# First norm, modulation and first projection of a two-layer backbone as a pipeline over channel tiles, in one written order per engine

## The chip, the cores and the metric

The kernel runs on one core of a Trainium2 chip. A core has TensorE (matrix products, PE in the rows; PEld is its load of the stationary operand), VectorE (DVE), ScalarE (ACT), GpSimd (POOL) and SyncE (SP), which here only issues DMAs. The metric is the device time of one execution in microseconds (us), as the median of several runs.

## What is computed

The reference is a backbone of two layers over 256 context tokens and 1024 latent tokens, 1024 channels wide. Only its beginning matters here:

```python
def modulate(x, shift, scale):
    return rmsnorm(x) * (1.0 + scale) + shift
...
    for layer in range(DEPTH):
        mod_l = (jax.nn.silu(c) @ w_ada[layer] + b_ada[layer])[:, None, :]
        mod_c = (jax.nn.silu(c_ctx) @ w_ada[layer] + b_ada[layer])[None, None, :]
        sh1_l, sc1_l, g1_l, sh2_l, sc2_l, g2_l = jnp.split(mod_l, 6, axis=-1)
        ...
        pl = split_proj(modulate(xl, sh1_l, sc1_l) @ w_in[layer])
        pc = split_proj(modulate(xc, sh1_c, sc1_c) @ w_in[layer])
        mixed = (hgrn2_mixer(...), mlstm_mixer(...), retention_mixer(...), gla_mixer(...))
        ...
```

`rmsnorm` divides each token by the root mean square over its 1024 channels. Four mixers (chunkwise scans), an output projection and an MLP follow in each layer.

## The kernel before

The tokens lie along the free axis, 1280 of them (256 context, then 1024 latent), in three blocks `TBS` of 256, 512 and 512; the channels lie on the partitions, in `NK` = 8 channel tiles of 128. The residual is `self.X[k]`, a tile of 128 x 1280 for each channel tile k (`x` in the rows). The normed, modulated input is kept as a sum of two parts of reduced precision, `Hhi` and `Hlo`, and weights likewise (hi and lo), so that each product of the projections is three matrix products: hi by hi, hi by lo, lo by hi. For most projections these are L294, L295 and L296 (`mm3`).

The program begins with `build`: the context block of x is loaded by ScalarE's queue, and the silu of the two conditions is made (`params`). Then the 16 tiles of shift and scale of the first norm (`mod`) come as one piece: `ada_unit` (L383) loads 32 pieces of `w_ada` (256 KB each, 512 columns) and multiplies each at once, `ada_finish` copies, transposes and adds the bias. `params2` and `cond_rows` make small tables for the mixers (some 40 operations on 4 to 24 columns).

`mix_open` then runs the first norm and the first projection of a layer. That projection is `denseVS` (L601): for each of `NC` = 10 chunks of 128 tokens it sums over the 8 channel tiles into one bank of PSUM, 304 columns wide, 3 products for each channel tile, 240 in all. ScalarE and VectorE evacuate a chunk (L604, L605). The eight weight tiles come from `w_vs`, and are split into hi on ScalarE (L591) and lo on VectorE (L592). In layer 0 the norm of each token block is `norm_mod`: `rstd` squares the eight channel tiles on ScalarE (L447), sums them by products with a tile of ones (L448, L452) and makes the inverse root by Ln and Exp (L454, L455; in its other form, where `fast` is 0, the squares L435 are summed by VectorE, L436, and one product L438 sums over the partitions; L440 and L441 are its Ln and Exp). `norm_apply` does three operations for each channel tile k of the block:

```python
            nc.vector.scalar_tensor_tensor(t, self.X[k][...], self.mod[...], r, ...)         # L477
            nc.scalar.activation(R(hi), t, AF.Identity, bias=b)                              # L480
            nc.vector.scalar_tensor_tensor(R(lo), t, b, hi, op0=ALU.add, op1=ALU.subtract)   # L482
```

The order of the instructions on each engine isn't that of the code: a scheduler of the tile framework sets it, from dependencies and a model of costs, and each engine then takes its instructions in that order. DMAs are issued by SP's queue in its order.

After the first projection, `turn` transposes part of its result (L616, evacuated by L617), and the mixers begin: small products and gates for the first mixer (L787, then L307 to L314), and beside them, as filler for TensorE, the other projections (L294 to L296, with weights split by L282 and L283).

## Time and profile before

| | |
|---|---|
| median of 3 runs | 3275.53 us (3268.72 to 3275.95) |
| the profiled execution | 3272.16 us |
| its span, from the first to the last instruction | 3270.4 us |
| PE busy | 3189.2 us (98%) |
| PEld busy | 2612.7 us (80%) |
| DVE busy | 2098.0 us (64%) |
| ACT busy | 1285.5 us (39%) |
| mean granted clock of TensorE | 0.992 |

An execution's time is a little longer than its span. Busy times are those of one profiled execution. A stretch of the granted clock is given as a share of 2.4 GHz: 1.00 is that, 0.50 is 1.2 GHz. Records of TensorE overlap, so a product's record is longer than its share of time; where many follow each other, the distance of their starts is what one costs. A product of 32-bit operands (the sums of squares, the modulation) has two records.

### The profile page before, as it was taken

The page shows a single profiled execution, that of the slowest core. Times are in us where ns is not written, and L with a number is a line of the kernel's source. Part 1 is how long each engine was busy: PE and PEld are TensorE (multiplying, and loading weights), DVE is VectorE, ACT ScalarE, POOL GpSimd, SP SyncE. Part 2 cuts the span into 40 slices and gives each one's busy share as a digit, 9 for nine tenths or more (in the row PEclk, how much of TensorE's full clock was granted, in tenths as well). Part 3 has the DMA queues.
Part 4 walks back from the last instruction along what each step waited for, and adds up shares of the span by engine and source line. Part 5 has one row for each costly group of instructions (what it writes and reads, how often), then busy time and mean ns, then how long its engine had stood idle before and what let it go on. Part 6 is the DMA issues. An engine that isn't in the chain of part 4 may idle for free.

```text
span 3270.4 us, 52561 instructions
## 1 busy us (share of the span) xinstructions
PE 3189.2 (98%) x20681; PEld 2612.7 (80%) x20681; DVE 2098.0 (64%) x4333; ACT 1285.5 (39%) x2665; POOL 11.5 (0%) x42
## 2 busy tenths in 40 slices
PE   7999999999999999999999999999999999999998
PEld 4787788877888888888888677788778888888887
DVE  4778887776588845454545586876756555555546
ACT  4666564546332121212122575764544322222222
POOL 0000000000000000000000000000000000000000
PEclk9999899999999999999999999999999999999999
DMA  5115565345157511111111222333324111111111
GB/s 208 60 60 178 180 187 195 117 135 183 57 164 232 161 39 39 39 39 39 39 39 40 78 66 71 118 108 115 94 71 149 58 48 49 46 52 46 52 49 65
DMA packets 181953, 308.20 MB, mean 94 GB/s; under 512 B 21880, under 2 KB 51240, under 8 KB 181448
## 3 DMA queue, kind: packets, MB, share of 16 engines
q1 hardware_dynamic: 180376, 303.02, 28.7%
q8 instruction: 162, 2.65, 0.3%
q10 hardware_dynamic: 1296, 1.81, 0.2%
q14 instruction: 87, 0.71, 0.1%
q0 software_dynamic: 32, 0.01, 0.0%
HBM read 259.11 MB, written 45.65 MB: 93 GB/s over the span
## 4 chain that ended last, share of the span: by engine, by line
PE 84%; DVE 6%; DMA 5%; ACT 3%; issue 1%; SPq 0%; DVEq 0%; ACTq 0%
PE psum L294 22%; PE psum L295 22%; PE psum L296 22%; PE psum L831 2%; PE psum L601 2%; PE psum L632 1%; PE psum L834 1%; PE psum L818 1%; PE psum L634 1%; PE psum L633 1%; PE psum L1019 1%; PE psum L706 1%; DMA ph<-w_adaR 1%; PE psum L1358 1%; DVE px L991 1%
## 5 line engine op out<-in xcount | busy, mean ns | idle before, releaser
L526 DVE SCALAR_TENSOR_TENSOR x<-psum,st,x 128x512 f32<-128x512 f32 (+1 forms) x648 | 440.4, 689 | 204.3 <-PE psum L296 203.8
L282 ACT ACTIVATE pc<-st 128x512 fp32r<-128x512 f32 x256 | 161.3, 632 | 853.5 <-PE psum L295 841.3
L295 PE MATMUL psum<-pc,pc 128*128 128x512 f32 (+1 forms) x1296 | 477.1, 368 | 5.0 <-DVE pc L506 5.0
L294 PE MATMUL psum<-pc,pc 128*128 128x512 f32 (+1 forms) x1296 | 476.3, 368 | 0.0
L296 PE MATMUL psum<-pc,pc 128*128 128x512 f32 (+1 forms) x1296 | 474.9, 366 | 0.0
L294 PE MATMUL psum<-Hhi,pc 128*128 128x512 f32 (+1 forms) x1280 | 471.1, 368 | 1.6 <-ACT pc L282 1.5
L295 PE MATMUL psum<-Hlo,pc 128*128 128x512 f32 (+1 forms) x1280 | 472.0, 369 | 0.1
L296 PE MATMUL psum<-Hhi,pc 128*128 128x512 f32 (+1 forms) x1280 | 470.5, 368 | 0.0
L294 PE MATMUL psum<-Hhi,pw 128*128 128x512 f32 (+1 forms) x1192 | 450.8, 378 | 8.3 <-ACT pw L282 3.9
L296 PE MATMUL psum<-Hhi,pw 128*128 128x512 f32 (+1 forms) x1192 | 447.5, 376 | 0.6 <-DVE pw L283 0.6
L295 PE MATMUL psum<-Hlo,pw 128*128 128x512 f32 (+1 forms) x1192 | 446.5, 375 | 0.0
L505 DVE TENSOR_TENSOR st<-st 128x256 f32<-128x256 f32 (+1 forms) x160 | 101.8, 636 | 301.5 <-ACT pc L504 300.8
L295 PEld LDWEIGHTS psum<-pc,pc 128*128 128x128 f32 x1296 | 245.1, 189 | 47.0 <-DVE pc L506 5.5
L294 PEld LDWEIGHTS psum<-pc,pc 128*128 128x128 f32 x1296 | 245.1, 189 | 44.2 <-DVE x L526 1.3
L296 PEld LDWEIGHTS psum<-pc,pc 128*128 128x128 f32 x1296 | 244.7, 189 | 43.0 <-issue 2.7
L294 PEld LDWEIGHTS psum<-Hhi,pc 128*128 128x128 f32 x1280 | 241.3, 189 | 43.3 <-ACT pc L282 2.4
L295 PEld LDWEIGHTS psum<-Hlo,pc 128*128 128x128 f32 x1280 | 241.3, 189 | 40.9 <-issue 0.5
L283 DVE TENSOR_TENSOR pc<-st,pc 128x512 fp32r<-128x512 f32 x256 | 175.6, 689 | 153.3 <-ACT pc L282 133.4
L296 PEld LDWEIGHTS psum<-Hhi,pc 128*128 128x128 f32 x1280 | 241.1, 188 | 41.0 <-DVE pc L283 0.6
L294 PEld LDWEIGHTS psum<-Hhi,pw 128*128 128x128 f32 x1192 | 227.3, 191 | 54.4 <-issue 9.6
L296 PEld LDWEIGHTS psum<-Hhi,pw 128*128 128x128 f32 x1192 | 227.2, 191 | 39.4 <-issue 2.6
L295 PEld LDWEIGHTS psum<-Hlo,pw 128*128 128x128 f32 x1192 | 227.6, 191 | 37.2 <-issue 2.2
(401 smaller groups left out, 4868.6 us busy)
## 6 DMA issues: line engine op xcount, KB each, us to landing
st<-w_ff SPq DMA_DIRECT2D x256, 256.0 KB
ph<-w_adaR SPq DMA_DIRECT2D x128, 256.0 KB
st<-w_inT SPq DMA_DIRECT2D x96, 256.0 KB
st<-w_adaR SPq DMA_DIRECT2D x74, 256.0 KB
pc<-w_adaR SPq DMA_DIRECT2D x54, 256.0 KB
st<-w_out SPq DMA_DIRECT2D x50, 256.0 KB
d_z<-st SPq DMA_DIRECT2D x40, 256.0 KB
ps<-w_ada SPq DMA_DIRECT2D x32, 256.0 KB
```

Of the source, the lines that this page charges most:

```text
L282: nc.scalar.activation(hi, raw, AF.Copy)
L283: (eng or nc.vector).tensor_tensor(lo, raw, F(hi), op=ALU.subtract)
L294: t.matmul(out, lhsT=w[0], rhs=m[0], start=first, stop=False)
L295: t.matmul(out, lhsT=w[0], rhs=m[1], start=False, stop=False)
L296: t.matmul(out, lhsT=w[1], rhs=m[0], start=False, stop=last)
L505: nc.vector.tensor_tensor(r, r, r, op=ALU.mult)
L526: nc.vector.scalar_tensor_tensor(x, ps, self.mod[:, l, 40 + o, j:j + 1], x, op0=ALU.mult, op1=ALU.add)
L601: t.matmul(ps[:, 0:304], lhsT=h[a], rhs=u[b], start=(k + i == 0), stop=(k == NK - 1 and i == 2))
L632: t.matmul(ps[:, e, :], lhsT=h[0], rhs=u[0], start=(k == 0), stop=False)
L633: t.matmul(ps[:, e, :], lhsT=h[0], rhs=u[1], start=False, stop=False)
L634: t.matmul(ps[:, e, :], lhsT=h[1], rhs=u[0], start=False, stop=(k == NK - 1))
L831: nc.tensor.matmul(o, lhsT=ST[r0:r0 + kd, c, d, :], rhs=qd[d](c)[r0:r0 + kd, :], start=(j == 0), stop=False, tile_position=(r0, 0))
```

## The change

In layer 0, the modulation, the norm and the first projection become one function, `open_first`, written in the order in which each engine is to run it: the block `manual_schedule` keeps the code's order on every engine for what stands in it. The projection's inner piece is taken out as `part(c, k, bank)`: three products of chunk c with channel tile k; the loop over k is now outside the loop over the chunks, so six banks of PSUM are summed side by side. The first two token blocks (768 tokens, chunks 0 to 5) go through together: for each pair q of channel tiles come the quarter of the modulation that they need (`w_ada` is laid out anew, in four quarters of 8 pieces of 256 KB), two weight tiles, the norm's three operations (now L428, L430, L431) and the products (L665). The third block follows as a second pass over k with chunks 6 to 9. All loads are issued by SP. The sums of squares use `rstd` in its other form for all three blocks (its squares are now L508 and L511, its adds L512, its product L514, its Ln and Exp L516 and L517). `params2` and `cond_rows` are called at the end of `mix_open`. In layer 1 the same instructions come as before.

```diff
-    def ada_unit(self, l, r, k, bank, bufs):
...
-    def ada_finish(self, l, r, bank, bank2, tmp):
...
+    def open_first(self, vs):
+        nc, io, hp = self.nc, self.io, self.heap
+        aring = Ring([hp.alloc(512) for _ in range(10)])
+        two = CTX + 512
+        rs = {}
+        def load_x(a, b):
+            for k in range(NK):
+                nc.sync.dma_start(self.X[k][:, a:b], io["xT"][:, k, a:b])
+        def load_w(q):
+            out = []
+            for k in range(NK):
+                w = aring.next()(4, 128)
+                nc.sync.dma_start(w, io["w_ada"][q, k])
+                out.append(w)
+            return out
+        def products(ws):
+            for k in range(NK):
+                for g in range(4):
+                    nc.tensor.matmul(self.bank(6)[32 * g:32 * g + 32, 0:128], lhsT=self.cc[:, k, :], rhs=ws[k][:, g, :],
+                                     start=(k == 0), stop=(k == NK - 1), tile_position=(0, 32 * g))
+            s = self.tmps.items[6](128)
+            nc.scalar.activation(s, self.bank(6)[:, 0:128], AF.Copy)
+            return s
+        def shifts(q, s):
+            T = self.bank(7)[:, 0:128]
+            nc.tensor.transpose(T, s, self.ident)
+            T = T.rearrange("p (g j) -> p g j", j=32)
+            for e in range(2):
+                o = 8 * e + 2 * q
+                bb = self.bada[:, 0, o:o + 2].unsqueeze(2).to_broadcast([128, 2, 2])
+                nc.vector.tensor_tensor(self.mod[:, 0, o:o + 2, :], T[:, 2 * e:2 * e + 2, 0:2], bb, op=ALU.add)
+            m = self.mod[:, 0, 8 + 2 * q:10 + 2 * q, :]
             nc.vector.tensor_scalar(m, m, 1.0, None, op0=ALU.add)
+        def rms(tb, bank):
+            self.banks = Ring((bank,))
+            rs[tb] = self.rstd(tb)
+        def apply(k, tb):
+            t0, n = tb
+            j = 0 if t0 < CTX else 1
+            t = self.tN.next()(n)
+            b = self.mod[:, 0, k, j:j + 1]
+            hi, lo = self.Hhi[:, k, t0:t0 + n], self.Hlo[:, k, t0:t0 + n]
+            nc.vector.scalar_tensor_tensor(t, self.X[k][:, t0:t0 + n], self.mod[:, 0, 8 + k, j:j + 1], rs[tb],
+                                           op0=ALU.mult, op1=ALU.mult)
+            nc.scalar.activation(R(hi), t, AF.Identity, bias=b)
+            nc.vector.scalar_tensor_tensor(R(lo), t, b, hi, op0=ALU.add, op1=ALU.subtract)
+        with self.tc.manual_schedule():
+            load_x(0, two)
+            ws = load_w(0)
+            self.params(self.tmps.items[5])
+            rms(TBS[0], 0)
+            rms(TBS[1], 1)
+            s = products(ws)
+            shifts(0, s)
+            vs.pre(2)
+            ws = load_w(1)
+            apply(0, TBS[0])
+            apply(0, TBS[1])
+            for q in range(4):
+                k = 2 * q
+                for c in range(6):
+                    vs.part(c, k, c)
+                apply(k + 1, TBS[0])
+                apply(k + 1, TBS[1])
+                if q < 3:
+                    s = products(ws)
+                    vs.pre(k + 4)
+                    if q < 2:
+                        ws = load_w(q + 2)
+                    else:
+                        load_x(two, NT)
+                for c in range(6):
+                    if c == 3 and q < 3:
+                        shifts(q + 1, s)
+                    vs.part(c, k + 1, c)
+                if q < 3:
+                    apply(k + 2, TBS[0])
+                    apply(k + 2, TBS[1])
+            rms(TBS[2], 7)
+            last = (6, 0, 1, 7)
+            for c in range(6):
+                vs.evac(c, c)
+            for k in range(NK):
+                apply(k, TBS[2])
+                for c in range(6, NC):
+                    vs.part(c, k, last[c - 6])
+            for c in range(6, NC):
+                vs.evac(c, last[c - 6])
+        hp.free(*aring.items)
+        self.banks = Ring(range(8))
...
-    def norm_mod(self, l, tbs, sh, sc):
...
+        def part(c, k, bank):
+            h, u = self.hm(k, 128 * c, 128), vs.h[k]
+            for i, (a, b) in enumerate(((0, 0), (0, 1), (1, 0))):
+                t.matmul(self.bank(bank)[:, 0:304], lhsT=h[a], rhs=u[b], start=(k + i == 0), stop=(k == NK - 1 and i == 2))
+
+        def evac(c, bank):
+            ps = self.bank(bank)
+            nc.scalar.activation(V[:, c, :], ps[:, 0:256], AF.Copy)
+            nc.vector.tensor_copy(P[:, c, :], ps[:, 256:304])
+
         def body(w):
             for c in range(NC):
-                ps = self.bank(self.dbanks.next())
+                bank = self.dbanks.next()
                 for k in range(NK):
-                    h, u = self.hm(k, 128 * c, 128), w[k]
-                    for i, (a, b) in enumerate(((0, 0), (0, 1), (1, 0))):
-                        t.matmul(ps[:, 0:304], lhsT=h[a], rhs=u[b], start=(k + i == 0), stop=(k == NK - 1 and i == 2))
+                    part(c, k, bank)
                     if k == 3:
                         yield 1500
-                nc.scalar.activation(V[:, c, :], ps[:, 0:256], AF.Copy)
-                nc.vector.tensor_copy(P[:, c, :], ps[:, 256:304])
+                evac(c, bank)
                 yield 1500
-        return Dense(load, NK, body)
+        vs = Dense(load, NK, body)
+        vs.part, vs.evac = part, evac
+        return vs
...
         vs = self.denseVS(self.gl, self.sp)
-        vs.pre(NK)
         if l == 0:
-            for t0, n in TBS[1:]:
-                for k in range(NK):
-                    self.nc.sync.dma_start(self.X[k][:, t0:t0 + n], self.io["xT"][:, k, t0:t0 + n])
-        gen = iter(vs)
-        blocks = self.norm_mod(l, TBS, 0, 8) if l == 0 else iter(TBS)
-        if l == 1:
+            self.open_first(vs)
+        else:
+            vs.pre(NK)
+            gen = iter(vs)
             self.norm_block(l, TBS[-1], 0, 8, fast=FAST[3])
-        for (t0, n), _ in zip(TBS, blocks):
-            for _ in range(n // 64):
-                next(gen, None)
-        next(gen, None)
+            for _ in gen:
+                pass
         self.poolX.release()
         px, xs = self.pool(f"px{l}", [nx], side="right")
         hp.add(xs[0])
         hp.add(self.tR.items[0])
         self.mix_pools, self.pw = (ph, px), pw
+        if l == 0:
+            self.params2(self.tmps.next())
+            self.cond_rows(self.tmps.next())
...
     b.openX()
-    for k in range(NK):
-        nc.scalar.dma_start(b.X[k][:, 0:CTX], io["xT"][:, k, 0:CTX])
-    b.params(b.tmps.next())
-
-    ps, ss = b.pool("ps", [512] * 16)
-    bk = b.banks.next()
-    ring = Ring(ss)
-    for k in range(NK):
-        b.ada_unit(0, 0, k, bk, ring)
-    b.ada_finish(0, 0, bk, b.banks.next(), b.tmps.next())
-    ps.release()
-    b.params2(b.tmps.next())
-    b.cond_rows(b.tmps.next())
...
-    A["w_ada"] = ca(w_ada[:1, :, :2048].reshape(1, 8, 128, 1, 4, 512).transpose(0, 3, 1, 2, 4, 5))
+    A["w_ada"] = ca(w_ada[0, :, :2048].reshape(8, 128, 2, 4, 256).transpose(3, 0, 1, 2, 4).reshape(4, 8, 128, 4, 128))
```

The places in the order that matter below. VectorE, third token block, before (L477 and L482 are the first and third operation of the norm, `x_4_89` is channel tile 4, L605 an evacuation):

```order
L477 SCALAR_TENSOR_TENSOR st<-x_2_87,st 128x512
L605 COPY ph_0_256<-psum 128x48
L477 SCALAR_TENSOR_TENSOR st<-x_3_88,st 128x512
L482 SCALAR_TENSOR_TENSOR Hlo<-st,Hhi 128x512
L477 SCALAR_TENSOR_TENSOR st<-x_4_89,st 128x512
L482 SCALAR_TENSOR_TENSOR Hlo<-st,Hhi 128x512
L477 SCALAR_TENSOR_TENSOR st<-x_5_90,st 128x512
L605 COPY ph_0_256<-psum 128x48
L482 SCALAR_TENSOR_TENSOR Hlo<-st,Hhi 128x512 x2
L477 SCALAR_TENSOR_TENSOR st<-x_6_91,st 128x512
```

VectorE, the same block now (L428 and L431 are these operations):

```order
L428 SCALAR_TENSOR_TENSOR st<-x_0_85,st 128x512
L431 SCALAR_TENSOR_TENSOR Hlo<-st,Hhi 128x512
L428 SCALAR_TENSOR_TENSOR st<-x_1_86,st 128x512
L431 SCALAR_TENSOR_TENSOR Hlo<-st,Hhi 128x512
L428 SCALAR_TENSOR_TENSOR st<-x_2_87,st 128x512
L431 SCALAR_TENSOR_TENSOR Hlo<-st,Hhi 128x512
L428 SCALAR_TENSOR_TENSOR st<-x_3_88,st 128x512
L283 TENSOR_TENSOR pw_0_96<-st,pw_0_96 128x512
L431 SCALAR_TENSOR_TENSOR Hlo<-st,Hhi 128x512
```

Before, an L477 of a further tile stands between L477 and L482 of one tile at most places; now L431 stands right behind its L428, but for tiles 3, 5, 6 and 7, where a weight's lo part (L283) or small operations of `params2` come between.

VectorE now at the border from the first to the second pair of channel tiles (L659 makes the lo part of a weight tile, L414 and L416 the shifts and scales of the pair):

```order
L428 SCALAR_TENSOR_TENSOR st<-x_1_86,st 128x256
L431 SCALAR_TENSOR_TENSOR Hlo<-st,Hhi 128x256
L428 SCALAR_TENSOR_TENSOR st<-x_1_86,st 128x512
L431 SCALAR_TENSOR_TENSOR Hlo<-st,Hhi 128x512
L659 TENSOR_TENSOR pw_0_96<-st,pw_0_96 128x304 x2
L414 TENSOR_TENSOR st<-psum,st 128x4 x2
L416 TENSOR_SCALAR st<-st 128x4
L428 SCALAR_TENSOR_TENSOR st<-x_2_87,st 128x256
L431 SCALAR_TENSOR_TENSOR Hlo<-st,Hhi 128x256
L428 SCALAR_TENSOR_TENSOR st<-x_2_87,st 128x512
L431 SCALAR_TENSOR_TENSOR Hlo<-st,Hhi 128x512
```

The same alternation stands in the first two blocks, with nothing between L428 and L431; two L659 and three small operations stand at the border. ScalarE at the same border (L430 is the norm's second operation, L403 copies a quarter of the modulation out of PSUM, L658 makes the hi part of a weight tile):

```order
L430 ACTIVATE Hhi<-st 128x256
L430 ACTIVATE Hhi<-st 128x512
L430 ACTIVATE Hhi<-st 128x256
L430 ACTIVATE Hhi<-st 128x512
L403 ACTIVATE st<-psum 128x128
L658 ACTIVATE pw_0_96<-st 128x304 x2
L430 ACTIVATE Hhi<-st 128x256
L430 ACTIVATE Hhi<-st 128x512
L430 ACTIVATE Hhi<-st 128x256
```

L403 and L658 of a quarter stand behind the L430 of the pair before. There was no such place before: all of the modulation came ahead of the norm. ScalarE's sums of squares, before (L447; L480 is the norm's second operation):

```order
L447 ACTIVATE st<-x_7_92 128x256
L451 ACTIVATE st<-psum 128x256
L454 ACTIVATE st<-psum,st 128x256
L455 ACTIVATE st<-st 128x256
L389 ACTIVATE st<-psum 128x512
L591 ACTIVATE pw_0_252<-st 128x304 x4
L447 ACTIVATE st<-x_0_85 128x512
L480 ACTIVATE Hhi<-st 128x256
L447 ACTIVATE st<-x_1_86 128x512
L591 ACTIVATE pw_0_252<-st 128x304
```

and now (L508 and L511 are squares of the first block up to `x_7_92 128x256`, then of the second; L516 and L517 are Ln and Exp):

```order
L511 ACTIVATE st<-x_6_91 128x256
L511 ACTIVATE st<-x_7_92 128x256
L516 ACTIVATE st<-psum,st 128x256
L517 ACTIVATE st<-st 128x256
L508 ACTIVATE st<-x_0_85 128x512
L511 ACTIVATE st<-x_1_86 128x512
L511 ACTIVATE st<-x_2_87 128x512
L511 ACTIVATE st<-x_3_88 128x512
```

The squares of the second block stood among the norm of the first; now they stand behind the first block's Exp, and ahead of any norm.

On TensorE the transposes (now L692) and 14 products of L294 to L296 (512 columns each), which stood behind the whole first projection, now stand inside its third block.

## Rows read from the trace of the kernel before

**Rows 1.** Page, part 4: the chain that ended last, by engine.
```profile
PE 84%; DVE 6%; DMA 5%; ACT 3%; issue 1%; SPq 0%; DVEq 0%; ACTq 0%
```

**Rows 2.** Stretches: length, busy time of each engine (instructions), clock, DMA share, GB/s.
```profile
0.00:6.00 6.00, 0.00 (x0) 0.00 (x0) 0.40 (x3) 1.28 (x1) 0.20 (x4) 1.00 0.65 208
6.00:10.00 4.00, 0.00 (x0) 0.00 (x0) 0.00 (x0) 0.00 (x0) 0.00 (x0) 1.00 1.05 392
...
89.00:280.00 191.00, 186.92 (x2063) 149.06 (x2062) 149.39 (x380) 116.75 (x262) 0.00 (x0) 1.00 0.26 85
```

**Rows 3.** TensorE's timeline, end of the first projection: start, us, instruction.
```profile
87.59 0.30 PE L601 MATMUL psum<-pw,Hlo 128*128 128x304 f32 x1
...
88.01 0.30 PE L601 MATMUL psum<-pw,Hlo 128*128 128x304 f32 x1
88.15 0.93 PE L616 MATMUL psum<-st,ph 128*48 128x128 f32 x7
...
89.68 0.36 PE L294 MATMUL psum<-Hhi,pw 128*128 128x256 f32 x1
```

**Rows 4.** Three lines of the norm: duration in ns, minimum, median, maximum.
```profile
L477 DVE SCALAR_TENSOR_TENSOR st<-x,st x88: 476/743/752, 35.6 to 2568.7; 128x512 f32<-128x512 f32 x64, 128x256 f32<-128x256 f32 x24
L480 ACT ACTIVATE Hhi<-st x88: 491/723/730, 36.1 to 2569.5; 128x512 fp32r<-128x512 f32 x64, 128x256 fp32r<-128x256 f32 x24
L482 DVE SCALAR_TENSOR_TENSOR Hlo<-st,Hhi x83: 472/742/753, 37.2 to 2570.7; 128x512 fp32r<-128x512 f32 x59, 128x256 fp32r<-128x256 f32 x24
```

**Rows 5.** Timelines of VectorE and ScalarE in the norm of layer 0.
```profile
43.29 0.49 ACT L480 ACTIVATE Hhi<-st 128x256 fp32r<-128x256 f32 x1
...
43.81 0.48 DVE L482 SCALAR_TENSOR_TENSOR Hlo<-st,Hhi 128x256 fp32r<-128x256 f32 x1 [1.00 <-ACT Hhi L480]
44.21 0.48 DVE L477 SCALAR_TENSOR_TENSOR st<-x,st 128x256 f32<-128x256 f32 x1
...
65.59 0.74 DVE L477 SCALAR_TENSOR_TENSOR st<-x,st 128x512 f32<-128x512 f32 x1
66.25 0.74 DVE L482 SCALAR_TENSOR_TENSOR Hlo<-st,Hhi 128x512 fp32r<-128x512 f32 x1
66.92 0.74 DVE L477 SCALAR_TENSOR_TENSOR st<-x,st 128x512 f32<-128x512 f32 x1
...
66.37 0.72 ACT L480 ACTIVATE Hhi<-st 128x512 fp32r<-128x512 f32 x1 [0.60 <-DVE st L477]
```

**Rows 6.** Sums of squares elsewhere, by line (ns) and timeline; two dependent VectorE operations.
```profile
L435 ACT ACTIVATE st<-x x49: 402/632/637, 810.7 to 3242.5; 128x512 f32<-128x512 f32 x35, 128x256 f32<-128x256 f32 x14
L436 DVE TENSOR_TENSOR st<-st x49: 415/689/694, 811.5 to 3243.3; 128x512 f32<-128x512 f32 x35, 128x256 f32<-128x256 f32 x14
L440 ACT ACTIVATE st<-psum,st x7: 476/688/693, 834.4 to 3245.2; 128x512 f32<-128x512 f32 x5, 128x256 f32<-128x256 f32 x2
...
3244.11 1.09 PE L438 MATMUL psum<-st 128*128 128x512 f32 x2
...
131.54 0.69 DVE L732 TENSOR_TENSOR_SCAN st<-st 128x256 f32<-128x256 f32 x1
132.27 0.42 DVE L733 TENSOR_TENSOR st<-st 128x256 f32<-128x256 f32 x1
```

**Rows 7.** VectorE's timeline: two lo parts of weight tiles.
```profile
39.33 0.86 DVE L592 TENSOR_TENSOR pw<-st,pw 128x304 fp32r<-128x304 f32 x2 [0.48 <-ACT pw L591]
```

**Rows 8.** TensorE's clock: L383 from 14 and from 27 us; a stretch as in rows 2.
```profile
L383 PE MATMUL psum<-ps,st x16: 647/1057/1060, 14.3 to 16.9; 128*32 128x512 f32 x16
...
L383 PE MATMUL psum<-ps,st x18: 592/592/617, 26.6 to 30.0; 128*32 128x512 f32 x18
...
334.00:351.00 17.00, 11.71 (x47) 7.96 (x47) 12.52 (x28) 7.20 (x15) 0.00 (x0) 0.51 0.23 73
```

**Rows 9.** Stretches as in rows 2: the mixers of layer 0; dense products alone.
```profile
89.00:720.00 631.00, 605.91 (x5637) 488.09 (x5636) 513.34 (x1343) 359.50 (x847) 1.54 (x14) 0.98 0.45 142
...
840.00:880.00 40.00, 40.00 (x175) 32.49 (x174) 19.36 (x32) 12.51 (x20) 0.00 (x0) 1.00 0.12 40
```

More of the change, by code (lines that the diff above doesn't have):

```diff
@@ L375, in params2 @@
         nc.scalar.activation(self.o["rtd"](24), lg, AF.Exp, scale=128.0)
-    def ada_unit(self, l, r, k, bank, bufs):
-        nc = self.nc
-        for g in range(4):
-            w = bufs.next()(512)
-            nc.sync.dma_start(w, self.io["w_ada"][l, r, k, :, g, :])
-            nc.tensor.matmul(self.bank(bank)[32 * g:32 * g + 32, :], lhsT=self.cc[:, k, :], rhs=w,
-                             start=(k == 0), stop=(k == NK - 1), tile_position=(0, 32 * g))
-    def ada_finish(self, l, r, bank, bank2, tmp):
-        nc = self.nc
-        s = tmp(512)
-        nc.scalar.activation(s, self.bank(bank), AF.Copy)
-        T = self.bank(bank2).rearrange("p (c q) -> p c q", q=128)
-        for cb in range(4):
-            nc.tensor.transpose(T[:, cb, :], s[:, cb * 128:(cb + 1) * 128], self.ident)
-        Tv = self.bank(bank2).rearrange("p (c g j) -> p g c j", g=4, j=32)[:, :, :, 0:2]
-        mo = self.mod[:, l, 16 * r:16 * r + 16, :].rearrange("p (g c) j -> p g c j", c=4)
-        bb = self.bada[:, l, 16 * r:16 * r + 16].rearrange("p (g c) -> p g c", c=4)
-        nc.vector.tensor_tensor(mo, Tv, bb.unsqueeze(3).to_broadcast([128, 4, 4, 2]), op=ALU.add)
-        if r in (0, 2):
-            a = 8 if r == 0 else 32
-            m = self.mod[:, l, a:a + 8, :]
-            nc.vector.tensor_scalar(m, m, 1.0, None, op0=ALU.add)
@@ L456, in rstd @@
         return r
-    def norm_mod(self, l, tbs, sh, sc):
-        rs = [self.rstd(tbs[0], FAST[0])]
-        for i, tb in enumerate(tbs):
-            if i + 1 < len(tbs):
-                rs.append(self.rstd(tbs[i + 1], FAST[0]))
-            self.norm_apply(l, tb, rs[i], sh, sc)
-            yield
     def norm_block(self, l, tb, sh, sc, eng=None, fast=False):
```

## The prediction

> **What bounds the kernel now.** I read the page first. TensorE holds 84% of the chain that ended last [rows 1], so a change pays only where it lets TensorE start its work sooner or stand still less. I then cut the span into stretches: TensorE has no work at all in the first 10 us, and from 89 to 280 us it is busy for 187 of 191 us [rows 2]. So the question is one of place: when does TensorE reach the point at which the mixers' projections feed it without a gap? Before, the first projection's last product (L601) starts at 88.01 us and ends by 88.15, the transposes (L616) and one short product (L787) follow, and at 89.68 us the stream of L294 begins [rows 3]. I compare with these two times.
>
> For the cost of one piece I read lines singly. Of the norm, a channel tile of 256 tokens takes 0.48 us on VectorE (L477), 0.49 on ScalarE (L480), 0.48 on VectorE (L482); a tile of 512 takes 0.74, 0.72, 0.74 [rows 4]. The timelines add three things. A hop from one engine to the other costs 0.03 to 0.04 us (65.59 + 0.74 to 66.37; 43.29 + 0.49 to 43.81). VectorE may begin the next independent instruction after 0.66 us of a 512 tile and 0.40 us of a 256 tile. And in the order of before, where L477 of the next tile stands ahead of L482 of this one, a 512 tile costs 1.33 us (L477 at 65.59 and 66.92), though its three operations need 2.2 us one behind the other [rows 5].
>
> **The change, step by step.** What leaves: 32 loads of a whole modulation before anything else, 24 products for the sums of squares (L448), and the scheduler's order. What comes: the modulation in four quarters, each followed by two channel tiles of the first two token blocks; sums of squares by adds on VectorE; and one order on each engine. The order shown above matters most: on VectorE L428 and L431 of the same tile now stand next to each other, so every L431 waits for ScalarE's L430, and nothing can be put into that wait.
>
> Row 43.81 of [rows 5] shows what such a place costs: VectorE stood idle for 1.00 us before L482, and an L477 was behind it. The Trainium skill, "TensorE: Matmul & The Clock Gate", in its section on the array of 32×32 parts, says that ScalarE and VectorE run strictly in the order of their queue; that rule speaks against this change, and the row fits it.
>
> One channel tile of the two blocks then costs (0.48 + 0.04 + 0.49 + 0.03 + 0.40) + (0.74 + 0.04 + 0.72 + 0.03 + 0.66) = 1.44 + 2.19 = 3.6 us, and one of the third block 2.2 us, where the order of before took 1.33.
>
> *Start.* 4.1 MB (constants, parameters, the first 768 tokens) come first. Up to 6 us 208 GB/s arrived, then 392 [rows 2]: 1.25 MB by 6 us, the rest 7.3 us later, 13.3; with the last landing I take 14. Block 1: last square 0.4, add 0.42, product 0.95 (half of block 2's, below), Ln and Exp 0.9, hops 0.2: 16.9. Block 2's squares stand on ScalarE behind that Exp. Its seven adds depend on each other, at 0.69 + 0.04 each (131.54 to 132.27 shows the 0.04): two squares 1.2, adds 5.1, product 1.9 (1.09 at the high clock; low here), Ln 0.69, Exp 0.63 like a square: 9.5, so 26.5 [rows 6]. The first quarter's 32 short products stand on TensorE behind the product that ends at 25.1. Of L383, 16 records, two to a product, began within 2.6 us at the low clock [rows 8]: 0.33 us a product of 512 columns, so 0.08 for 128 columns, 2.6 us a quarter here and 1.3 at the high clock; since the start of a product does not shrink with it, I take 1.8 for the latter. Copy, transpose, three small adds, two weight halves (0.39 each, from 0.86 for two [rows 7]): VectorE begins the first tile at about 30 us.
>
> *Loop of four quarters.* 8 × 3.6 = 29. At three borders VectorE also does two weight halves and three small adds (1.3), and waits some 0.5 us for ScalarE, whose copy of the products (L403) and two L658 stand behind the last L430: 1.85 each, 5.5 in all. End: 30 + 29 + 5.5 = 64.5. TensorE needs 36 × 0.14 + 1.8 + 0.2 = 7 us of each 9.1 (three L601, from 87.59 to 88.01, take 0.42 [rows 3]), and a quarter's 2.4 MB take 6.2 us at 392 GB/s: neither is the bound.
>
> *Third block.* Its squares stand behind the last L430, its adds behind the last L431: again about 8.7, to 73. Six copies (L669) and six L670 behind the Exp: 2. The first L430 then waits for two L693, which wait for TensorE's transposes: its L431 ends near 79. Seven more tiles at 2.2, plus 1 us for L283 and the small operations of params2 where they don't fit into the wait of 0.75: 95.5; the last tile's products 1.5 to 2: 97. TensorE is idle for most of 66 to 77 us. After such a hole its clock falls: before, it ran at 0.51 from 334 to 351 us, in which it was busy for 11.7 us [rows 8]. A tile's 12 products then take 3.0 instead of 1.7 us, longer than VectorE's 2.2. I put 0.5 for it, included.
>
> *Back in step.* Behind the last product come evacuation, three transposes, L863 twice: 3.5 us until L294 streams, against 89.68 - 88.15 = 1.5 before. But by then 14 products of L294 to L296 have been done inside the third block (175 of them fill 40 us, 0.23 each [rows 9]: 3.2) and one L863 more (1.1). So the same work is reached at 97 + 3.5 - 4.3 = 96.2 instead of 89.7: 6.5, say 7 us later. The removed L448 products save TensorE time that it spent waiting anyway. The moved params2 (some 40 small operations of VectorE) had lain under the loads; now most lie in VectorE's waits, and what is left (2 us) delays the first gate features, which TensorE covers with two dense tiles (48 × (0.23 + 0.23 + 0.12) = 28 us).
>
> Bounds of the sum. Low: the data 1.5 us earlier, the start at the high clock (products 0.5, 0.95 and 0.8 less), no clock loss in the third block (0.5), all of params2 hidden (1): 97 - 5.3 = 91.7, so +1 or +2. High: from 78 us on, TensorE at the low clock for 17 us, as from 334 to 351; of the 8 × 1.7 + 3.2 = 16.8 us of work it does 8.5, the rest takes 8.3: 103, so +13.
>
> *After it.* The mixers of layer 0 have another order too, since the scheduler starts from another state and the heap hands out other addresses; from the first MLP on the orders agree. In 89 to 720 us TensorE is idle for 25 us, with a mean clock of 0.98 [rows 9], and I see no reason in the new order for more or less. I take 0, with some 8 us either way; one hole like that of 334 to 351 costs 5.3 idle and 5.8 of half speed, 11 us.
>
> **Sum.** The profiled execution took 3272.2 us (span 3270.4), the median of the three runs is 3275.5. 3272.2 + 7 = 3279 for an execution like the profiled one, and 3282 for the median. About 0.3% (9.8 us) is what a measurement of this kernel can tell from no change.
>
> **Rivals.**
>
> *The waits are hidden (faster).* If VectorE's rate, not the round trip through ScalarE, were the pace, a tile would cost 2.1 us in the loop and 1.33 in the third block: 12 and 6 us less, with the rest of the sum the projection ends near 79 and the total is 3282 - 18 = 3264. For it: 1.33 is what the trace has now. Against it: that pace needs another instruction between L428 and L431, and the new order has none in the loop. The point from which it decides is a saving of 17 us. 8%.
>
> *The mixers' new order loses a hole (faster).* The hole at 334 to 351 goes away: 3282 - 11 = 3271, and with the sum at its low end 3265. 10%, half of it faster.
>
> *The mixers' new order gains a hole (slower).* One more like it: 3293. For it: VectorE is busy for 513 of 631 us there [rows 9], and 12.5 of the 17 us of that hole, in which TensorE was busy for 11.7 [rows 8]. 15%.
>
> *TensorE stays at the low clock in the loop (slower).* Its share of work there is 7 in 9.1. At the low clock a quarter would need 13 us and TensorE would be the bound: 4 × 4 = 16 more, 3298. For it: the first products ran at half speed (1057 ns against 592 later [rows 8]) from 14.3 to 16.9 us, and 69% busy went with the low clock from 334 to 351. Against it: as the bound TensorE would be busy without a gap, and so it was from 840 to 880 us, at the high clock [rows 9]. The Trainium skill, same page, section on what is actually happening, says that the low clock is the default and activity releases it; these rows agree. 10%.
>
> *The forecast*, with its end between +1 and +13: 57%, of which 12 end beyond 9.8 us.
>
> **Chances.** Faster 8 + 5 = 13%. Slower 12 + 15 + 10 = 37%. Same 45 + 5 = 50%. The likeliest case alone spans 3276 to 3289; eight in ten reach from 3264, the two faster cases, to 3297, the two slower ones.
>
> **What would show it.** Right: L428 and L431 alternate with about 0.75 us idle before each 512-token L431, released by L430; a quarter takes about 9 us; TensorE does nothing for several us around 70; the last L665 ends between 91 and 104 us; the clock is low somewhere in 68 to 90. Wrong: the last L665 before 85 us (the waits are hidden) or after 108 (the clock); or a total that differs while the last L665 stands where I say, which would put the cause into the mixers of layer 0, up to 720 us.

## The result: slower by 1.1%, and the profile after

| | before | after |
|---|---|---|
| median, us (runs) | 3275.74 (4; 3268.72 to 3286.57) | 3315.78 (4; 3311.98 to 3324.56) |
| ratio to before, 95% interval | | 1.0112 [1.0092, 1.0133] |
| the profiled execution, us (span) | 3272.16 (3270.4) | 3314.04 (3312.3) |
| mean granted clock of TensorE | 0.992 | 0.983 |

By the medians the change costs 40 us, by the ratio 37, and the time is above the forecast range of 3264 to 3297. Where in the program do they arise? The page of the changed kernel first, part 4, to compare with [rows 1]:

```profile
PE 79%; DVE 10%; DMA 6%; ACT 3%; issue 1%; SPq 0%; DVEq 0%; ACTq 0%
```

VectorE has four points more of the chain, TensorE five fewer. The stretches, with the columns of [rows 2], show two places:

```profile
0.00:40.00 40.00, 14.61 (x164) 10.63 (x165) 15.42 (x33) 17.48 (x35) 0.20 (x4) 0.96 0.69 254
40.00:80.00 40.00, 28.73 (x254) 22.27 (x252) 23.46 (x50) 17.37 (x35) 0.00 (x0) 0.88 0.49 170
...
320.00:360.00 40.00, 33.25 (x383) 26.42 (x379) 37.41 (x97) 27.29 (x64) 0.00 (x0) 0.91 0.55 171
358.00:388.00 30.00, 18.74 (x120) 13.15 (x119) 20.75 (x51) 15.07 (x32) 0.15 (x1) 0.55 0.19 64
...
400.00:440.00 40.00, 34.92 (x294) 24.56 (x293) 32.42 (x95) 21.33 (x53) 0.21 (x2) 0.82 0.63 200
```

One is the opening, as expected. The other is a place that the change doesn't touch: from 358 to 388 us, in the middle of layer 0's mixers, TensorE is busy for 18.7 of 30 us, at a mean clock of 0.55. The hole of before in that neighbourhood was 17 us long ([rows 8], last row).

The opening first. VectorE's timeline, the loop, its first border and the third block:

```profile
29.50 0.48 DVE L428 SCALAR_TENSOR_TENSOR st<-x,st 128x256 f32<-128x256 f32 x1
30.56 0.48 DVE L431 SCALAR_TENSOR_TENSOR Hlo<-st,Hhi 128x256 fp32r<-128x256 f32 x1 [0.58 <-ACT Hhi L430]
30.96 0.75 DVE L428 SCALAR_TENSOR_TENSOR st<-x,st 128x512 f32<-128x512 f32 x1
32.49 0.75 DVE L431 SCALAR_TENSOR_TENSOR Hlo<-st,Hhi 128x512 fp32r<-128x512 f32 x1 [0.79 <-ACT Hhi L430]
33.16 0.48 DVE L428 SCALAR_TENSOR_TENSOR st<-x,st 128x256 f32<-128x256 f32 x1
...
36.15 0.75 DVE L431 SCALAR_TENSOR_TENSOR Hlo<-st,Hhi 128x512 fp32r<-128x512 f32 x1 [0.79 <-ACT Hhi L430]
39.02 0.86 DVE L659 TENSOR_TENSOR pw<-st,pw 128x304 fp32r<-128x304 f32 x2 [2.12 <-ACT pw L658]
...
40.30 0.48 DVE L428 SCALAR_TENSOR_TENSOR st<-x,st 128x256 f32<-128x256 f32 x1
...
67.31 0.75 DVE L431 SCALAR_TENSOR_TENSOR Hlo<-st,Hhi 128x512 fp32r<-128x512 f32 x1 [0.79 <-ACT Hhi L430]
68.36 5.47 DVE L512 TENSOR_TENSOR st<-st 128x512 f32<-128x512 f32 x7 [0.29 <-ACT st L511]
77.54 1.58 DVE L670 COPY ph<-psum 128x48 f32<-128x48 f32 x6 [3.71 <-ACT ph L669]
79.03 0.74 DVE L428 SCALAR_TENSOR_TENSOR st<-x,st 128x512 f32<-128x512 f32 x1
81.64 0.75 DVE L431 SCALAR_TENSOR_TENSOR Hlo<-st,Hhi 128x512 fp32r<-128x512 f32 x1 [1.87 <-ACT Hhi L430]
...
98.64 0.75 DVE L431 SCALAR_TENSOR_TENSOR Hlo<-st,Hhi 128x512 fp32r<-128x512 f32 x1
```

Read the two waits in brackets: 0.58 and 0.79 us before every L431 of the loop, both released by ScalarE's L430. A tile takes 33.16 - 29.50 = 3.66 us. What follows on TensorE and ScalarE, to compare with [rows 3]; the first mixer's first product is the row with 56 instructions:

```profile
101.16 0.30 PE L665 MATMUL psum<-pw,Hlo 128*128 128x304 f32 x1
...
103.88 0.39 PE L294 MATMUL psum<-Hhi,pw 128*128 128x256 f32 x1
...
105.07 0.69 ACT L307 ACTIVATE st<-psum,st 128x512 f32<-128x512 f32 x1 [1.11 <-DVE st L372]
...
138.86 1.72 PE L894 MATMUL psum<-ph 128*32 128x64 f32 x56 [2.63 <-ACT ph L970]
```

The last product of the first projection starts at 101.16 instead of 88.01 us, and TensorE stands still for 2.63 us before the first mixer's product, where it had 0.22 us of wait before:

```profile
125.98 1.03 PE L818 MATMUL psum<-ph,px 128*32 128x64 f32 x56 [0.22 <-ACT px L894]
```

The mixers' hole, TensorE's timeline of the changed kernel:

```profile
357.96 0.40 PE L296 MATMUL psum<-Hhi,pw 128*128 128x512 f32 x1
360.87 1.87 PE L1032 MATMUL psum<-st,px 128*128 128x2 f32 x8 [2.52 <-DVE px L1028]
365.06 1.87 PE L1032 MATMUL psum<-st,px 128*128 128x2 f32 x8 [2.32 <-DVE px L1011]
369.18 0.69 PE L910 MATMUL psum<-px 128*64 128x128 f32 x4 [2.26 <-ACT px L1120]
...
384.39 1.08 PE L1095 MATMUL psum<-px,ph 128*32 128x64 f32 x32 [2.60 <-DVE px L1067]
385.60 0.79 PE L294 MATMUL psum<-Hhi,pw 128*128 128x512 f32 x1
```

Between 357.96 and 385.60 no dense product (L294 to L296) stands in TensorE's order; it runs nothing but a mixer's chain, which goes to and fro with VectorE and ScalarE. Before, the dense products stopped at 331.3 and came again at 341.2 us.

### The profile page after: what moved, and what is told of

It is laid out like the page before. It is cut to its first block, busy times and chain, and to the rows that moved or that the text cites. A ratio compares the mean times of both kernels' runs of the same rounds, so it can differ in the third digit from the quotient of the medians.

```text
span 3312.3 us, 52881 instructions
## 1 busy us (share of the span) xinstructions
PE 3192.7 (96%) x20825; PEld 2626.3 (79%) x20825; DVE 2110.5 (64%) x4364; ACT 1288.4 (39%) x2665; POOL 11.5 (0%) x42
## 4 chain that ended last, share of the span: by engine, by line
PE 79%; DVE 10%; DMA 6%; ACT 3%; issue 1%; SPq 0%; DVEq 0%; ACTq 0%
PE psum L294 21%; PE psum L295 21%; PE psum L296 21%; PE psum L907 2%; PE psum L665 1%; PE psum L910 1%; PE psum L894 1%; PE psum L708 1%; PE psum L709 1%; DMA ph<-w_adaR 1%; PE psum L710 1%; PE psum L1095 1%; PE psum L782 1%; PE psum L1434 1%; DVE px L1067 1%
## 5 line engine op out<-in xcount | busy, mean ns | idle before, releaser
L294 PE MATMUL psum<-pc,pc 128*128 128x512 f32 (+1 forms) x1296 | 476.6, 368 | 0.0
L296 PE MATMUL psum<-pc,pc 128*128 128x512 f32 (+1 forms) x1296 | 475.2, 367 | 0.0
L294 PE MATMUL psum<-Hhi,pc 128*128 128x512 f32 (+1 forms) x1280 | 471.1, 368 | 1.5 <-ACT pc L282 1.5
L296 PE MATMUL psum<-Hhi,pc 128*128 128x512 f32 (+1 forms) x1280 | 470.5, 368 | 0.0
L294 PE MATMUL psum<-Hhi,pw 128*128 128x512 f32 (+1 forms) x1192 | 455.0, 382 | 2.9 <-ACT pw L282 1.3
L296 PE MATMUL psum<-Hhi,pw 128*128 128x512 f32 (+1 forms) x1192 | 446.9, 375 | 0.0
L294 PEld LDWEIGHTS psum<-pc,pc 128*128 128x128 f32 x1296 | 245.3, 189 | 44.2 <-DVE x L593 1.2
L296 PEld LDWEIGHTS psum<-pc,pc 128*128 128x128 f32 x1296 | 244.9, 189 | 43.0 <-issue 2.7
L294 PEld LDWEIGHTS psum<-Hhi,pc 128*128 128x128 f32 x1280 | 241.3, 189 | 43.3 <-ACT pc L282 2.4
L296 PEld LDWEIGHTS psum<-Hhi,pc 128*128 128x128 f32 x1280 | 241.1, 188 | 41.0 <-DVE pc L283 0.6
L283 DVE TENSOR_TENSOR pc<-st,pc 128x512 fp32r<-128x512 f32 x256 | 175.6, 690 | 153.2 <-ACT pc L282 133.4
L294 PEld LDWEIGHTS psum<-Hhi,pw 128*128 128x128 f32 x1192 | 227.5, 191 | 49.7 <-issue 9.3
L296 PEld LDWEIGHTS psum<-Hhi,pw 128*128 128x128 f32 x1192 | 227.3, 191 | 37.7 <-issue 2.3
```

Of the source, the lines that this page charges most:

```text
L283: (eng or nc.vector).tensor_tensor(lo, raw, F(hi), op=ALU.subtract)
L294: t.matmul(out, lhsT=w[0], rhs=m[0], start=first, stop=False)
L296: t.matmul(out, lhsT=w[1], rhs=m[0], start=False, stop=last)
```

## The experiments

Two places, so two suspects. **Theory:** the mixers' order of layer 0 follows from where their buffers lie. `open_first` takes ten slots of 512 words from the heap and gives them back, but the heap's cursor, from which later buffers are handed out, stays behind them; other buffers collide, and the scheduler places the dense products elsewhere. **Rival:** the opening's delay brings the holes, whatever the addresses. For the opening itself: the hand order on VectorE, the low clock of TensorE, the moved small operations, or the sums of squares.

Each kernel's marks, from its profiled execution: the norm's first operation on VectorE, the last product of the first projection, the first mixer's product (56 in a row), and the last evacuation of the output projection (x <- psum), all starts in us (in e5 the 56 products stand in two pieces). From the last mark on the instructions of TensorE, VectorE and ScalarE stand in the same order, but for a few of VectorE and ScalarE near 2570 us in before and e1, and some twenty places in layer 1 in e5 and e7. e2 and e10 are the same kernel and show how far a mark can be trusted: theirs are 0.1, 1.6, 1.8 and 0.9 us apart.

| kernel | ratio to before, 95% | norm | last product | mixer | output projection |
|---|---|---|---|---|---|
| before | | 35.62 | 88.01 | 125.98 | 916.5 |
| after | 1.0112 [1.0092, 1.0133] | 29.50 | 101.16 | 138.86 | 952.6 |
| e1 | 1.0066 [1.0041, 1.0091] | 37.09 | 90.90 | 128.83 | 939.6 |
| e2 | 1.0032 [1.0017, 1.0046] | 30.41 | 103.08 | 140.29 | 930.7 |
| e3 | 1.0002 [0.9987, 1.0018] | 30.47 | 91.07 | 130.05 | 918.4 |
| e4 | 0.9972 [0.9958, 0.9985] | 26.72 | 82.88 | 121.72 | 910.3 |
| e5 | 1.0087 [1.0068, 1.0107] | 41.34 | 111.70 | | 936.3 |
| e6 | 1.0067 [1.0049, 1.0085] | 30.47 | 97.76 | 136.12 | 931.5 |
| e7 | 0.9968 [0.9956, 0.9979] | 25.78 | 74.55 | 113.15 | 902.3 |
| e8 | 0.9956 [0.9942, 0.9970] | 21.69 | 72.00 | 110.55 | 900.9 |
| e9 | 1.0037 [1.0017, 1.0057] | 26.92 | 82.60 | 120.72 | 933.7 |
| e10 | 1.0027 [1.0015, 1.0039] | 30.52 | 101.52 | 138.53 | 931.7 |
| e11 | 1.0023 [1.0011, 1.0035] | 30.61 | 98.40 | 135.64 | 924.7 |

**e1: the old opening, the new addresses.**

```diff
         if l == 0:
+            hp.free(*[hp.alloc(512) for _ in range(10)])
             for t0, n in TBS[1:]:
```

> The kernel before, with ten heap slots of 512 taken and given back at the start of layer 0, so that the mixers' buffers lie where they lie in the changed kernel; the opening is the old one. Theory (addresses): the order of layer 0's mixers follows from these addresses, and holes like those at 336 to 343, 360 to 388 and 411 to 442 us of the changed kernel come with them: 3302 us (3294 to 3308), with a hole of TensorE over 20 us long between 320 and 440. Rival (opening): the holes come from the later start of the changed kernel, whatever the addresses: 3276 us (3270 to 3281), the only hole of that stretch the one that was there.

1.0066 [1.0041, 1.0091] is +22 us; the medians, 3298.67 and 3281.75 for the kernel before beside it, are 17 us apart. The hole is there, with the same waits as in the changed kernel. TensorE's waits in 310 to 440 us (in all, times, longest):

```profile
PE psum L1019 <- DVE px L991: 5.7, 3, 2.6
PE psum L1019 <- ACT st L308: 5.0, 1, 5.0
PE psum L956 <- DVE st L935: 2.3, 1, 2.3
PE psum L956 <- DVE px L935: 2.3, 1, 2.3
PE psum L956 <- DVE px L952: 2.3, 1, 2.3
```

The same view of the changed kernel, 325 to 455 us (the same instructions, 76 lines further down in the file):

```profile
PE psum L1095 <- DVE px L1067: 5.8, 3, 2.6
PE psum L1095 <- ACT st L308: 5.0, 1, 5.0
PE psum L1032 <- DVE px L1028: 2.5, 1, 2.5
PE psum L1032 <- DVE st L1011: 2.3, 1, 2.3
PE psum L1032 <- DVE px L1011: 2.3, 1, 2.3
```

**e2: the new opening, the old addresses.**

```diff
         hp.free(*aring.items)
+        hp.cur = (0, 0)
```

> The changed kernel with the heap's cursor set back to its start after the opening: the mixers' buffers lie, and their instructions stand, as in the kernel before. Theory (addresses): what is left is the opening, the last product of the first projection at about 101 us against 88: 3288 us (3283 to 3294), and the hole of 20 us and more in 350 to 390 is gone. Rival (opening): the late start brings the holes: 3315 us (3308 to 3320).

1.0032 [1.0017, 1.0046], and the mixers' order is that of before, with the waits of before. The largest three of e2 in 310 to 440 us:

```profile
PE psum L1033 <- DVE px L1012: 3.9, 1, 3.9
PE psum L1096 <- ACT px L1062: 2.0, 1, 2.0
PE psum L294 <- DVE st L728: 1.4, 1, 1.4
```

and of the kernel before in 300 to 430 us (its lines stand 77 further up):

```profile
PE psum L956 <- DVE px L935: 3.9, 1, 3.9
PE psum L1019 <- ACT px L985: 2.1, 1, 2.1
PE psum L294 <- DVE st L651: 1.4, 1, 1.4
```

The theory holds and the rival falls: either part of the change can be had without the other, and 0.66% + 0.32% make 0.98%, inside the interval of the whole. By the last mark e1 has +23.1, e2 +14.2, the changed kernel +36.0 us. From the first mixer's product to that mark, the nine kernels of the table with the old addresses and both marks take 788 to 795 us, the three with the new ones (the changed kernel, e1, e9) 811 to 814, whether the mixers start at 121 or at 139 us. In that stretch TensorE is idle for 39 to 41 us with the new addresses and for 25 to 34 with the old, at a mean clock of 0.96 beside 0.97 to 0.98: about half of the 22 us is idle time, and the rest goes with the clock. The order has a threshold, though only ten slots were run: in the programs with one to seven slots in e1's line every engine's order is that of before, with eight and nine it is e1's.

**e3: one tile of lead on VectorE.** L428 of the next tile ahead of L431 of this one, in the loop and in the third block:

```diff
+        late = []
+        def drain():
+            while late:
+                late.pop()()
...
             nc.scalar.activation(R(hi), t, AF.Identity, bias=b)
-            nc.vector.scalar_tensor_tensor(R(lo), t, b, hi, op0=ALU.add, op1=ALU.subtract)
+            drain()
+            late.append(lambda: nc.vector.scalar_tensor_tensor(R(lo), t, b, hi, op0=ALU.add, op1=ALU.subtract))
...
+                apply(k + 1, TBS[0])
                 for c in range(6):
                     vs.part(c, k, c)
-                apply(k + 1, TBS[0])
                 apply(k + 1, TBS[1])
+                drain()
...
+            apply(0, TBS[2])
             for k in range(NK):
-                apply(k, TBS[2])
+                if k + 1 < NK:
+                    apply(k + 1, TBS[2])
+                else:
+                    drain()
```

> As e2_after_old_addresses, but on VectorE the first operation of the next tile stands ahead of the last operation of this one, in the loop and in the third block. Theory (the round trip through ScalarE sets the pace, 3.66 us a tile in the loop and 2.2 in the third block): a tile costs 2.1 and 1.3 us on VectorE, TensorE's 7 us a quarter and 1.7 us a tile become the pace, and the last product of the first projection ends near 90 us instead of 101: 8 to 12 us less than e2, 3278 us (3274 to 3282). Rival (the quarter's modulation and TensorE's clock set the pace): within 3 us of e2.

The last product starts at 91.07 instead of 103.08 us, the total is 9.5 us below e2 (3280.25 and 3289.71 on the same chip). A tile of the third block now takes 78.42 - 77.09 = 1.33 us, with no wait at most places (one later tile waits 1.82 us):

```profile
77.09 0.75 DVE L434 SCALAR_TENSOR_TENSOR st<-x,st 128x512 f32<-128x512 f32 x1
77.75 0.75 DVE L438 SCALAR_TENSOR_TENSOR Hlo<-st,Hhi 128x512 fp32r<-128x512 f32 x1
78.42 0.75 DVE L434 SCALAR_TENSOR_TENSOR st<-x,st 128x512 f32<-128x512 f32 x1
```

**e4: the scheduler's order.**

```diff
         hp.free(*aring.items)
+        hp.cur = (0, 0)
...
-        with self.tc.manual_schedule():
+        if True:
```

> As e2_after_old_addresses, without the block that keeps the code's order: the scheduler places the same instructions. Theory (the hand order costs, not the pipeline): it staggers the tiles again and fills VectorE's waits, 8 to 12 us less than e2, 3278 us (3273 to 3283). Rival (the pipeline itself costs: a modulation in quarters, sums of squares by VectorE, three weight borders): within 3 us of e2, 3288.

More than expected: 19 us below e2, and faster than before, 0.9972 [0.9958, 0.9985]. The scheduler puts the lead in by itself, and in addition places the first quarter's products ahead of the product for the second block's sum of squares on TensorE, so that the norm starts 3.7 us earlier. The pipeline isn't what costs; its hand order is.

**e5: params2 and cond_rows at the start, in the hand order.**

```diff
             self.params(self.tmps.items[5])
+            self.params2(self.tmps.items[7])
+            self.cond_rows(self.tmps.items[7])
...
-            self.params2(self.tmps.next())
-            self.cond_rows(self.tmps.next())
+            self.tmps.next()
+            self.tmps.next()
```

> As e2_after_old_addresses, but params2 and cond_rows are called at the start, under the loads, as in the kernel before; the mixers' order stays that of before. Theory (the moved small operations delay the first gates: in e2 the first L307 stands 1.9 us idle for L373, and some of them lie between the third block's L431): the first L307 comes 2 to 3 us earlier against the last product of the first projection, and the total is 2 to 3 us below e2, 3287 us beside 3282 for the kernel before. Rival (all of it is covered): within 1 us of e2.

Neither: the norm starts 11 us later than in e2. The small operations, each of which needs the one before, hold VectorE from 7.3 to 16.6 us ahead of the adds, and ScalarE's second square waits 4.7 us more, probably because `cond_rows` sends its result out of the buffer into which the squares go. The edit has its own cost, so it doesn't price the place at the end; e7 and e8 do.

**e6: TensorE kept busy between the loop and the third block.**

```diff
...
+            keep(24)
             rms(TBS[2], 7)
+            keep(18)
...
```

`keep(n)` issues n products of resident operands into the free bank 6.

> As e2_after_old_addresses, with 24 spare products of 304 columns ahead of the third block's L514 and 18 behind it, whose results nobody reads, so that TensorE doesn't stand still between the loop and the third block. Theory (VectorE's round trips set the third block's pace and the low clock costs under a microsecond, as the forecast had it): within 1.5 us of e2. Rival (TensorE's low clock from 76 to 89 us costs): the clock stays at 1.00 there, the last L431 comes 3 us earlier, and the total is 3 to 4 us below e2.

The clock stays at 1.00 from 40 to 120 us, the last product starts 3.8 to 5.3 us earlier than in e10 and e2, the mixer's product 2.4 to 4.2. But at the output projection nothing is left (931.5 beside 931.7 and 930.7), and the ratio is above e2's and e10's (1.0067 beside 1.0032 and 1.0027, each measured on another chip beside the kernel before), which no trace here explains. The rival's first half holds, its total doesn't.

**e7 and e8: sums of squares early.** From e4. Squares and adds of blocks 1 and 2 side by side, those of block 3 in the loop; in e7 params2 at the start, in e8 at the end.

```diff
...
-            rms(TBS[0], 0)
-            rms(TBS[1], 1)
+            for a0, a1 in zip(sums(TBS[0], extra[:3]), sums(TBS[1], extra[3:])):
+                pass
+            root(TBS[0], a0, 0)
+            root(TBS[1], a1, 1)
...
+                    if q == 1:
+                        load_x(two, NT)
+                        third = sums(TBS[2], (self.tmps.items[5], aring.items[2], aring.items[3]))
...
+                if q == 2:
+                    for _ in range(3):
+                        next(third)
...
+                if q == 3:
+                    for a2 in third:
+                        pass
...
-            rms(TBS[2], 7)
+            root(TBS[2], a2, 7)
...
```

`sums` yields after each of its seven adds; `root` is the product, Ln and Exp; `extra` are six scratch tiles.

> As e4_scheduler_order, with params2 and cond_rows at the start, the squares and adds of the first two blocks side by side for each channel tile instead of one block behind the other, and those of the third block inside the loop. Theory (what is left of the opening's cost is VectorE's sums of squares ahead of the first tile and ahead of the third block): the first tile begins near 22 us instead of 26.7, the last product of the first projection ends near 68 instead of 82.9, 10 to 16 us below e4: ratio to the kernel before 0.992 to 0.994. Rival (the gates of the first mixer, or the modulation's quarters, set what comes next): within 3 us of e4, ratio 0.997.

> As e7_early_sums, but params2 and cond_rows stay at the end as in the changed kernel. Theory (they delay the first gates by 2 to 3 us, as in e5): 2 to 3 us above e7. Rival (covered): within 1 us of e7.

The last product comes at 74.55 and 72.00 us, 8 and 11 us before e4's, not the 15 that I expected. At the output projection e7 is 8.0 and e8 9.4 us ahead of e4, 0.3% of the whole, and the intervals of the three totals overlap. e8 is the fastest, 0.9956 [0.9942, 0.9970], and both beat the kernel before; but e7's 0.9968 is not the 0.992 to 0.994 of its theory, and e8, expected 2 to 3 us above e7, is not above it. From last product to mixer's product e7 takes 38.60 and e8 38.55 us: params2 at the end is covered. At the start it delays the norm by 4.1 us.

**e9: the changed kernel without the hand order, nothing else** (e4 without its first line).

> The changed kernel without the block that keeps the code's order, and nothing else: the heap's cursor stays where the ten slots left it. Theory (addresses and hand order are two separate costs that add): the opening of e4, the mixers of e1, so 20 to 24 us above e4: ratio to the kernel before 1.003 to 1.005, the last evacuation of the output projection at about 932 us. Rival (the mixers' holes come with the late start of the hand order): as e4, ratio 0.997, that evacuation at about 910 us.

As the theory said: 1.0037 [1.0017, 1.0057] and 933.7. The opening is e4's to 1 us, the hole of the new addresses is back (waits of 5.8, 5.0, 2.9, 2.3, 2.3, 2.3 us in 310 to 440), and costs 23.4 us between e4 and e9.

**e10 and e11: the clock in the loop.** e10 is e2's kernel as the base; e11 is e6 with `keep(4)` behind each channel tile's products.

> The kernel of e2_after_old_addresses once more, as the base for e11 on the same chip: ratio to the kernel before 1.002 to 1.006, first product of the first mixer (56 of them in a row) at about 140 us, last evacuation of the output projection at about 931 us.

> As e6_keep_busy, with four spare products also behind each channel tile's products in the loop, 32 more, so that TensorE has fewer gaps there. Theory (the low clock in the loop lengthened the borders from the forecast's 1.85 us to 3.5): the clock stays above 0.95 from 32 us on, the last L431 of the loop comes 2 to 3 us earlier than in e10, the first mixer's product 6 to 7 us earlier. Rival (the borders are long for another reason): the last L431 of the loop within 1 us of e10, or later by the spare products' own time. On the total: if what e6 lost again by 300 us is general, within 2 us of e10 at the last evacuation of the output projection; if not, 5 us less.

Stretches of TensorE (busy, instructions, clock, DMA), e10:

```profile
60.00:72.00 12.00, 7.92 (x46) 1.00 0.36 133
72.00:76.00 4.00, 2.08 (x2) 0.56 0.00 0
76.00:84.00 8.00, 4.38 (x11) 0.50 0.00 0
84.00:92.00 8.00, 7.56 (x43) 0.86 0.11 35
```

and e11:

```profile
60.00:72.00 12.00, 10.92 (x72) 1.00 0.34 124
72.00:76.00 4.00, 3.77 (x23) 1.00 0.02 4
76.00:84.00 8.00, 6.34 (x38) 1.00 0.00 0
84.00:92.00 8.00, 8.00 (x53) 1.00 0.09 33
```

The low clock is gone from 36 us on, but the loop's last L431 stands at 67.82 us beside 67.25: the spare products took as long as the clock gave, as the rival has it. What the low clock costs at a border shows between two traces of one kernel, e2 and e10: the third border is 1.5 us longer than the second in e2, where the clock is low from 55.2 to 58.7 us, and equal to it in e10, where the clock is 1.00. There ScalarE's copy (L403), and VectorE behind it, wait for TensorE's products of the quarter (L400), which take 2.58 us in e2 and 1.95 in e10. In the third block, from its first L431 to its last, it is 15.5 us at the high clock beside 17.3 (80.73 to 96.25; 81.69 to 99.00). The mixer's product comes 2.9 us earlier, not 6 to 7; the last mark is 7.0 us earlier, the totals overlap (1.0023 and 1.0027). So e6 and e11 disagree on what the earlier mixer is worth at the end, and that stays open; by these traces the clock in the opening is worth 2.4 to 4.2 us at the mixer's product and 7 at most at the last mark. The Trainium skill, "TensorE: Matmul & The Clock Gate", in its section on what is actually happening, has it that activity releases the clock; these two kernels agree (1.00 in both from 76 to 84 us, where e10 has 0.50).

## Why the prediction was wrong

**Right.** The norm's start (30 forecast, 29.50 measured); the tile (3.6; 3.66, with the waits that the forecast named); the sums of squares (0.73 forecast for an add and its hop; 5.47 us for seven, 0.78 each); the way into the third block (14.5 forecast from the end of the loop to the end of its first L431; 68.0 to 82.4, 14.4) and its pace (16.5 from there to the end of its last; 82.4 to 99.4, 17.0). That the last product came between 91 and 104 is in part luck: the upper end was made of 6 us for the low clock in the third block, which cost 1.8, and what took its place were the borders. e3 shows the round trip through ScalarE as the cause.

**The step that failed** is "After it": "I see no reason in the new order for more or less. I take 0, with some 8 us either way". The order rows showed that the mixers' order changed, and the forecast named why (other addresses), but it took the average of idle time in before (25 of 631 us) for that of any order. Shown by e1, e2 and e9: the addresses alone bring 21 to 23 us by the last mark. That is the rival "the mixers' new order gains a hole", which had 15%, with the right place and half the price: it counted one hole of 11 us; the new order has more of them between 336 and 442 us, and the one at 358 alone loses 30 - 18.7 = 11.3 us idle and 18.7 x 0.45, some 8 us, to the clock (an estimate). The prediction's last sign of being wrong names this case: a total that differs while the last L665 stands where it was said.

**Mis-sized: the opening.** Forecast +6.5, measured +13 to +15 (last product and mixer's product, changed kernel, e2 and e10). Two terms. The last product ends at 101.5, not 97: the loop ends at 68.0 instead of 64.5, since its borders took 3.5, 2.1 and 3.6 us instead of 1.85 each (the long ones at the low clock, which e2 and e10 price at 1.5 us for the third), and the rest is half a microsecond each in the third block's pace and behind its last L431. And "Back in step" added 2.0 us until L294 streams and took 4.3 off for products of L294 and L863 done early. There is no such credit at the mixer: from the last product to the first mixer's product it is 37.0 to 39.0 us in all twelve rows with that mark, whether the dense work ahead of it had begun or not. What waits is the chain of gates; dense products done early only make its cover shorter (the 2.63 us of wait). Without both the forecast's own 97 gives 97 - 88.15 = +8.9.

**The rivals.** "The waits are hidden" is refuted for the changed kernel, and e3 has its 1.33 us a tile at most places of the third block. "TensorE at the low clock in the loop" came in part: short stretches (33.1 to 36.5, 53.5 to 57.0 and 74.0 to 87.7 us), for some 3 us by the two long borders (an estimate: 1.5 at the third by e2 and e10, as much again at the first) and 1.8 in the third block (e11), not the 16 of that rival. The moved params2 (2 us of work left over, which the forecast took to be covered) costs nothing that e7 and e8 tell apart.

**Open:** which pair of colliding buffers moves the dense products; only that the addresses do it is shown. And how much of a gain in the opening survives to the end when the clock brings it (e6, e11), and why e6's ratio is 0.4% above e10's at an equal last mark.

## What to carry to other kernels

Scratch memory that is borrowed and given back is not neutral where an allocator keeps a cursor: compare the order of what comes behind, and if it changed, price it as unknown, by the largest hole that the old order shows and more, or put the cursor back and be rid of the question. In an order by hand, put the next tile's first operation between two operations that go through another engine; or leave that stretch to the scheduler, which here found it and 10 us more. Count a delay to the first instruction of the chain that is waited for, not to the filler beside it.

## What the runs showed of the hardware that was not expected

Behind the last mark, with the same instructions in the same order on every engine, an execution takes from 2351.9 (e3) to 2369.7 us (e8) to the end of its span: a spread of 18 us that no change here explains, and as large as most of the effects; the totals of e8 alone spread from 3252.2 to 3272.4. A mark in the trace, at the end of what the change can touch, told kernels apart that their totals could not (0.9 us between e2 and e10, the same kernel).

TensorE's low clock outlasted the wait that it came with: in the changed kernel it fell at the end of the first wait of 2.5 us, at 360.7 us, and stayed at 0.50 until 388.1 (0.55 on the mean from 358 to 388), though TensorE was busy for 18.7 of these 30 us, for the most part with products of 2 to 128 columns. And 74 spare products that nobody reads (42 x 0.14 and 32 x 0.14, some 10 us of work) made the kernel of e11 no slower than e10.
